# Four tiles of the input projection from attention's hosts into two mixed seven-product pairs

## The chip, the core and the metric

The kernel runs on one core of one Trainium2 chip, as one launch. The metric is the device time of the launch in microseconds. The core has TensorE (PE, matrix products into PSUM), VectorE (DVE), ScalarE (ACT), GpSimd (POOL), SyncE (SP, which here issues most of the DMAs), and 16 DMA engines that move data between device memory and SBUF.

## The reference, cut to what matters

One step of a streaming encoder layer on 1024 prompt frames and 32 sample frames, model width 1024, in float32:

```python
h = rms_norm(x, g_mix)
z = h @ w_in
q, k, v, ch, cb, cc, ga, gb = jnp.split(z, SPLITS, axis=-1)
a = attn_core(q, k, v) @ w_attn_out           # 16 heads of 64, 4 key heads, window of chunks, sink
u = cc * ch
up = jnp.concatenate([conv_left, u], axis=1)
conv = sum(up[:, j:j + n] * conv_w[j] for j in range(3))
bo = (cb * conv) @ w_conv_out
x = x + (jax.nn.sigmoid(ga) * a + jax.nn.sigmoid(gb) * bo) @ w_mix_out
x = x + memory_attention(rms_norm(x, g_cross))
x = x + jnp.square(jax.nn.relu(rms_norm(x, g_mlp) @ w_up)) @ w_down
```

The layer also returns the new keys and values and the last two rows of `u` (the conv state).

## The kernel before, in words

Activations lie transposed: 128 features in the partitions, frames in the free dimension. The 1056 frames are three chunks of 384, 384 and 288 (`CH`, chunks 0 to 2). The 1024 features are eight blocks of 128. A weight tile holds the 1024 input features of 128 output features, 512 KB.

Each float32 value is used as a high part (cast to fp32r by ACT) and a low part (what is left, by DVE). A block product is three matmuls: high by high, high by low, low by high. So a whole tile on one chunk is 8 x 3 = 24 matmuls (`gemm`, L195), and on the three chunks 72: 48 of 384 columns, 24 of 288. The casts and subtractions of a weight tile are L129 and L130 (`split`); `issue_w` (L164) makes them, with `fetch_w` (L147) loading the tile ahead through SP. For a few weight tiles that are used once per chunk the low part is written to device memory at the first use and read back later (`kept`, L1824; the write is L179, the read L172, and the high part is cast at L173).

The input projection has 50 such tiles: 8 of queries, 2 of keys (values apart), and 8 each of conv H, B and C, gate a and gate b. They are treated in two ways.

*Hosts.* Attention consists of 36 units (4 key heads by 9: eight blocks of 128 prompt queries and one of sample queries; `Unit`, L558). A unit has three steps: `scores` (products, then bias and maximum on DVE, exponentials on ACT, and the multiplication by the reciprocal sum, shared between ACT and DVE), `turn` (transposes on PE at L616, split into high and low), and `values` (products, then a sum). Whole tiles are laid between these steps, so that PE has work while DVE and ACT work on a softmax. These tiles are the hosts: a list of 20 at L765, three slots each (one per chunk). `begin` (L774) gives the slot in which each unit's scores start; its transposes come two slots later, its values three. Conv tiles of blocks 0 to 3, queries of key heads 1 to 3, the second key tile and gate a of block 0 are the hosts.

*Pairs.* The other conv tiles and gates go two output tiles at a time through a scheme with seven half products where eight are usual, on chunks 0 and 1. A product (L903) is 4 blocks x 3 matmuls of 384 columns, so a pair is 84 of these where two whole tiles have 96; chunk 2 is done plainly (`gate_c2`, L933), 24 matmuls of 288 for each tile. The scheme needs combinations of the activations, made beside the output products of attention, and combinations of the two tiles' weights. `CPAIRS` (L727) lists the conv pairs: C, H, B of blocks (4, 5), then of (6, 7). After them come seven pairs of gate a and gate b. In `conv_pair` (L1016) the six results of a pair come in a fixed order: first tile chunk 0, first tile chunk 2, second tile chunk 1, first tile chunk 1, second tile chunk 0, second tile chunk 2. `conv_C`, `conv_H` and `conv_B` take them: C is kept, H is multiplied by it to `u`, and B multiplies the three-tap sum of `u`.

*Weight sums.* POOL makes the weight combinations through `sum_step` (L740): it issues the load of the next half tile, then adds four times (L757) on the one before and issues its store. Two buffers take turns (`sum_tile`, L734): a tile of its own, and the space of `xacc`, in which sums of squares are gathered later. There are 62 pieces: 26 for the pairs, 32 for the down projection, 4 for the up projection. Steps are hung on the hosts (26 of them), on attention's output products, and on the pairs (three each). Their order among themselves is pinned; a timeline model at compile time sets how all other instructions of an engine are ordered between them.

*After the pairs* comes the trunk of chunk 0: eight conv_out tiles (`do_conv_out`, L1192, in which POOL adds the two branches, L1201, except in the last), conv_out tile 0 of chunk 1, and eight mix tiles (`do_mix`, L1207). Then the same for chunk 1 beside the cross attention of chunk 0, and so on.

The lines that the later steps touch: `open_att` (L456, opens attention's buffers), the softmax's multiplications (L606 on ACT, L608 on DVE), the conv state's writes (L681 and L1066), `load_a` (L959, loads attention's output for a gate), `do_attn_out` (L847: where the gate of a block is known, DVE multiplies and the product is stored; else ACT copies and the plain output is stored).

Of the kernel before, what the change touches and what calls it, by code (L numbers as in the profile page):

```python
# [10 lines left out]
F32 = mybir.dt.float32  # L11
# [7 lines left out]
P = 128  # L19
# [21 lines left out]
def hybrid_step(ctx: ExitStack, tc: tile.TileContext, io):  # L41
# [48 lines left out]
    usum_d = dram.tile([2, P, 2, 2, 512], F32, name="usum_d")  # L90
    gsum_d = dram.tile([13, P, 2, 2, 512], F32, name="gsum_d")
    a_d = spill("a_d")
# [362 lines left out]

    def open_att():  # L456
        closed(st_cm)
        A["cm"], A["pool"] = opened("att", bufs=1, reuse_waits="tile", side="right")
        A["cvt"] = A["pool"].tile([P, 4, 4], F32, name="cvt")

# [97 lines left out]
    class Unit:  # L558
# [5 lines left out]
        def scores(self):  # L564
# [39 lines left out]
            for h in range(G):  # L604
                if h < G // 2:
                    act.mul(stl[:, h, :nk], stl[:, h, :nk], rec[:, h : h + 1])  # L606
                else:
                    dve.tensor_scalar_mul(stl[:, h, :nk], stl[:, h, :nk], rec[:, h : h + 1])  # L608
# [31 lines left out]
    def do_conv(which, f, extras=()):  # L640
        def fn(w):
# [35 lines left out]
            if which == "H":  # L677
                pool_e.tensor_copy(A["cvt"][:, f, 0:2], u[:, 1024:1026])
                pool_e.tensor_copy(A["cvt"][:, f, 2:4], u[:, 1058:1060])
                if f == 3:  # L680
                    sp.dma_start(io["o_conv"][:, :4], A["cvt"])  # L681

# [43 lines left out]
    HBC = {"H": 0, "B": 1, "C": 2}  # L726
    CPAIRS = [(which, f) for f in (4, 6) for which in "CHB"]  # L727
    ptiles = [(10 + 8 * HBC[which] + f, 11 + 8 * HBC[which] + f) for which, f in CPAIRS]
    ptiles += [(34 + f, 42 + f) for f in PAIRS]
# [35 lines left out]
    hosts = []  # L765
    conv = [(which, f) for f in range(4) for which in "CHB"]
    take = lambda n: [conv.pop(0) for _ in range(n)]
    hosts += take(3) + [("Q", 1, 0), ("Q", 1, 1)]
    hosts += [("K", 1)] + take(2) + [("Q", 2, 0), ("Q", 2, 1)]
    hosts += take(3) + [("Q", 3, 0), ("Q", 3, 1)]  # L770
    hosts += take(4) + [("G", 0)]
    assert not conv and len(hosts) == 20

    begin = [[1, 2, 3, 5, 6, 8, 10, 11, 13]] + [[0, 1, 3, 5, 6, 8, 10, 11, 13]] * 2 + [[0, 1, 3, 4, 6, 7, 9, 10, 12]]  # L774
    slots = [[[], [], [], []] for _ in range(3 * len(hosts) + 1)]
    for kv in range(KV):
        o = 15 * kv
        slots[max(o - 2, 0)][2].append(lambda kv=kv: do_KS(kv))
        slots[o + 1][0].append(lambda kv=kv: do_KC(kv))
        for p in range(9):  # L780
            u = Unit(kv, p)
            at = o + begin[kv][p]
            slots[at][3].append(u.scores)
            slots[at + 2][1].append(u.turn)
            slots[at + 3][0].append(u.values)
    for i, h in enumerate(hosts):
# [8 lines left out]
        if h[0] == "Q":  # L795
            fn, key = do_Q(h[1], h[2], extras), qt(h[1], h[2])
        elif h[0] == "K":
            fn, key = do_K(h[1], extras), ("w_in", 8 + h[1])
        elif h[0] == "G":
            fn, key = do_gate(lambda c, t: sa.__setitem__((c, 0), t), extras), ("w_in", 34)  # L800
        else:
            fn, key = do_conv(*h, extras), conv_w(h[1], h[0])
# [175 lines left out]
    def conv_H(f, c, x, s):  # L978
        n = CH[c][1]
        t = ct2[f, c]  # L980
        u = cu[f, c] = slot(G["pool"], f"Gb{c}", n, F32)
        if s is None:
            dve.tensor_mul(u, x, t)
        else:
            dve.tensor_sub(u, x, s)
            dve.tensor_mul(u, u, t)
        if c == 2:
            pool_e.tensor_copy(cvt[0][:, f - 4, 0:2], u[:, 254:256])
            pool_e.tensor_copy(cvt[0][:, f - 4, 2:4], u[:, 286:288])

    def conv_B(f, c, x, s):
# [22 lines left out]
        sp.dma_start(bc_d[c][:, f], b)  # L1014

    def conv_pair(i):  # L1016
        which, f = CPAIRS[i]
        t1, t2 = ptiles[i]
        out = {"C": conv_C, "H": conv_H, "B": conv_B}[which]
        op = lambda kind: [gop[kind, k] for k in range(4)]  # L1020
        w1 = take_w(("w_in", t1))
        if i == 0:
# [3 lines left out]
            pump(4)  # L1026
        A1, B, C = (acc_tile([P, 384]) for _ in range(3))
        product(A1, w1, 0, op("b11"), True)
        s1 = Y["top"].tile([P, 384], F32, tag="s1", name=nm("s1"))
# [3 lines left out]
        product(A1, w1, 1, op("b21"), False)  # L1033
        out(f, 0, A1, None)
        pump(0)
        out(f, 2, gate_c2(w1), None)
        issue_w()
# [10 lines left out]
        product(B, w3, 0, op("n3"), False)  # L1048
        out(f + 1, 1, B, v)
        sum_step()  # L1050
        product(C, w4, 1, op("b22"), False)
        out(f, 1, C, u2)
        issue_w()
        fetch_w()
        w2 = take_w(("w_in", t2))
        product(B, w2, 1, op("n4"), False)
        out(f + 1, 0, B, s1)
        sum_step()
        issue_w()
        fetch_w()  # L1060
        out(f + 1, 2, gate_c2(w2), None)
        if i == len(CPAIRS) - 1:
            load_a(1, 0)
            load_a(1, 2)
        if which == "H" and f + 1 == NF - 1:
            sp.dma_start(io["o_conv"][:, 4:], cvt[0])  # L1066
# [756 lines left out]
    for name, n in (("w_conv_out", NF), ("w_mix", NF), ("w_cq", 2), ("w_co", 2)):  # L1823
        kept.update(((name, j), None) for j in range(1, n, 2) if (name, j) not in (("w_conv_out", 3), ("w_conv_out", 5)))  # L1824

# [355 lines left out]
```

## Time and profile before

| what | value |
|---|---|
| device time, median of 3 runs | 1732.54 us (1732.36 to 1736.21) |
| profiled execution | 1732.39 us |
| its span, first to last instruction | 1730.6 us |
| attention with its 20 hosts | 83.5 to 405.3 us |
| gate b of block 0, three short products, then attention's output products | 405.3 to 518.9 us |
| six conv pairs, seven gate pairs | 518.9 to 784.9 us |
| conv_out and mix of chunk 0 | 784.9 to 857.0 us |
| DMA traffic | 365.48 MB, mean 211 GB/s |

The page gives busy times and the costliest groups; the windows view gives busy times by stage, the granted PE clock and the DMA share; the timeline gives single instructions with the idle time before them and what ended it (`[1.83 <-DMA ...]`). Matmuls are pipelined: a matmul of 384 columns is drawn with 0.34 us, but the next one starts about 0.17 us after it, so costs are read from start to start.

### The profile page before, as it was taken

The numbers are of one execution on the slowest core, as the hardware profiler recorded it, in microseconds if no ns is written. First come the engines' busy times: TensorE is split into PE (matmuls) and PEld (weight loads), VectorE is DVE, ScalarE is ACT, GpSimd is POOL, SyncE is SP. The second block draws the span as 40 slices with busy tenths as digits, with TensorE's granted clock in tenths as the row PEclk, the third lists the DMA queues.
The fourth block names the chain that finished last, engine by engine and source line by source line (L and its number), as shares of the span: only waits on it lengthen the run. The fifth ranks groups of instructions, "written<-read, shape, count | busy, mean of one in ns | idle before, by whom it ended". The sixth has DMA issues, their size and how long they took to land.

```text
span 1730.6 us, 32544 instructions
## 1 busy us (share of the span) xinstructions
PE 1711.4 (99%) x12166; PEld 1694.8 (98%) x12166; DVE 1221.3 (71%) x2282; ACT 892.8 (52%) x1748; POOL 643.9 (37%) x731
## 2 busy tenths in 40 slices
PE   9999999999999999999999999999999999999998
PEld 8999999999999999999999999999999999999998
DVE  7788797986647776546777889787666686555675
ACT  8676666665223223434556676765444463433444
POOL 0024667675445554462225142106565410000122
PEclk9999999999999999999999999999999999999999
DMA  5334444547886768877766667776666695555554
GB/s 187 99 110 153 128 153 158 173 147 245 277 308 228 255 228 284 283 251 242 260 210 202 223 229 257 239 247 212 223 219 220 212 324 184 192 185 174 191 172 162
DMA packets 185566, 365.48 MB, mean 211 GB/s; under 512 B 19760, under 2 KB 102352, under 8 KB 185280
## 3 DMA queue, kind: packets, MB, share of 16 engines
q1 hardware_dynamic: 165376, 296.37, 51.8%
q0 software_dynamic: 19408, 66.27, 11.1%
q8 instruction: 95, 1.56, 0.4%
q10 hardware_dynamic: 624, 0.77, 0.1%
q14 instruction: 63, 0.52, 0.1%
HBM read 263.31 MB, written 99.43 MB: 210 GB/s over the span
## 4 chain that ended last, share of the span: by engine, by line
PE 42%; DMA 5%; DVE 3%; ACT 1%; issue 1%; POOL 0%; DVEq 0%; ACTq 0%; SPq 0%; POOLq 0%
PE acc L1954 5%; PE acc L1952 5%; PE acc L1953 5%; PE acc L908 4%; PE acc L909 4%; PE acc L910 4%; PE acc L202 2%; PE acc L200 2%; PE acc L201 2%; PE pc L908 2%; PE pc L910 2%; PE pc L909 2%; DMA wr<-wsum_d 1%; DVE wl L130 1%; DMA ct<-m_d 1%
## 5 line engine op out<-in xcount | busy, mean ns | idle before, releaser
L129 ACT CAST wh<-wr 128x1024 fp32r<-128x1024 f32 (+1 forms) x226 | 236.4, 1046 | 397.6 <-PE acc L1953 119.8
L130 DVE TENSOR_TENSOR wl<-wr,wh 128x1024 fp32r<-128x1024 f32 (+1 forms) x226 | 290.8, 1287 | 109.6 <-ACT wh L129 108.2
L287 POOL TENSOR_TENSOR xacc<-xacc,ct 128x384 f32<-128x384 f32 (+1 forms) x55 | 75.1, 1370 | 361.7 <-ACT ct L285 359.9
L200 PE MATMUL acc<-X,wh 128*128 128x384 f32 (+1 forms) x576 | 188.3, 327 | 0.0
L201 PE MATMUL acc<-X,wh 128*128 128x384 f32 (+1 forms) x576 | 187.2, 325 | 0.5 <-DVE X L291 0.5
L202 PE MATMUL acc<-X,wl 128*128 128x384 f32 (+1 forms) x576 | 186.0, 323 | 0.0
L200 PE MATMUL acc<-Y,wh 128*128 128x384 f32 (+1 forms) x432 | 140.6, 325 | 1.9 <-DVE ct L1200 1.9
L202 PE MATMUL acc<-Y,wl 128*128 128x384 f32 (+1 forms) x432 | 140.1, 325 | 1.8 <-DMA wl<-wl_d 1.8
L201 PE MATMUL acc<-Y,wh 128*128 128x384 f32 (+1 forms) x432 | 140.0, 324 | 0.0
L757 POOL TENSOR_TENSOR xacc<-xacc 128x256 f32<-128x256 f32 x124 | 110.2, 889 | 7.1
L201 PEld LDWEIGHTS acc<-X,wh 128*128 128x128 f32 x576 | 108.5, 188 | 2.1 <-DVE X L291 0.8
L200 PEld LDWEIGHTS acc<-X,wh 128*128 128x128 f32 x576 | 108.4, 188 | 0.8
L202 PEld LDWEIGHTS acc<-X,wl 128*128 128x128 f32 x576 | 108.4, 188 | 0.7
L757 POOL TENSOR_TENSOR ws<-ws 128x256 f32<-128x256 f32 x124 | 103.0, 831 | 7.4
L1954 PE MATMUL acc<-n,wl 128*128 128x264 f32 x352 | 100.1, 285 | 0.2 <-DVE wl L130 0.2
L1952 PE MATMUL acc<-n,wh 128*128 128x264 f32 x352 | 100.3, 285 | 0.0
L1953 PE MATMUL acc<-n,wh 128*128 128x264 f32 x352 | 100.2, 285 | 0.0
L200 PEld LDWEIGHTS acc<-Y,wh 128*128 128x128 f32 x432 | 81.7, 189 | 2.8 <-DVE ct L1200 2.8
L202 PEld LDWEIGHTS acc<-Y,wl 128*128 128x128 f32 x432 | 81.7, 189 | 2.1 <-DMA wl<-wl_d 2.1
L201 PEld LDWEIGHTS acc<-Y,wh 128*128 128x128 f32 x432 | 81.6, 189 | 0.0
L599 ACT ACTIVATE S<-S,nmx 128x257 f32<-128x257 f32 (+1 forms) x132 | 64.4, 490 | 25.8 <-DVE nmx L594 24.8
L908 PE MATMUL acc<-n,wh 128*128 128x264 f32 x256 | 72.9, 285 | 0.0
(474 smaller groups left out, 5999.1 us busy)
## 6 DMA issues: line engine op xcount, KB each, us to landing
wr<-in_w_up SPq DMA_DIRECT2D x53, 512.0 KB, 4.3
wr<-in_w_in SPq DMA_DIRECT2D x52, 512.0 KB, 4.0
wr<-wsum_d SPq DMA_DIRECT2D x40, 512.0 KB, 3.5
wr<-gsum_d SPq DMA_DIRECT2D x26, 512.0 KB, 4.5
wr<-in_w_conv_out SPq DMA_DIRECT2D x24, 512.0 KB, 4.1
wr<-in_w_mix SPq DMA_DIRECT2D x24, 512.0 KB, 4.9
wr<-in_w_down SPq DMA_DIRECT2D x24, 512.0 KB, 3.6
n_d<-Z SPq DMA_DIRECT2D x32, 264.0 KB, 4.3
```

Of the source, the lines that this page charges most:

```text
L129: act.copy(hi, src)
L130: dve.tensor_sub(lo, src, hi.bitcast(F32))
L200: pe.matmul(out, wh[:, a], hi, start=(k == 0), stop=False)
L201: pe.matmul(out, wh[:, a], lo, start=False, stop=False)
L202: pe.matmul(out, wl[:, a], hi, start=False, stop=(k == len(acts) - 1))
L757: pin(pool_e.tensor_tensor(t[:, to], t[:, x], t[:, y], op=ALU.add))
L908: pe.matmul(acc, wh[:, a], hi, start=(start and k == 0), stop=False, skip_group_check=True)
L909: pe.matmul(acc, wh[:, a], lo, start=False, stop=False, skip_group_check=True)
L910: pe.matmul(acc, wl[:, a], hi, start=False, stop=(k == 3), skip_group_check=True)
L1952: pe.matmul(a, wh[:, s], hi, start=(t == 0 and k == 0), stop=False, skip_group_check=True)
L1953: pe.matmul(a, wh[:, s], lo, start=False, stop=False, skip_group_check=True)
L1954: pe.matmul(a, wl[:, s], hi, start=False, stop=(t == 1 and k == 7), skip_group_check=True)
```

## The change

- The hosts are 16 instead of 20: C, H and B of block 3 and gate a of block 0 leave the list. `begin` packs a key head's nine units into 12 slots instead of 15. The very first unit has three slots before its transposes instead of two.
- Two pairs stand ahead of the six: (C of block 3, H of block 3), and (B of block 3, gate a of block 0). They bring four more pieces for POOL. `conv_pair` takes a kind for each of its two tiles. In the first new pair, H on chunk 1 comes before C on chunk 1, so its multiplication is put off until C is there (`late`). Gate a is multiplied by attention's output, loaded at the start of its pair (`gate_a`).
- The conv state of block 3 is stored by SP from `u` itself, instead of through POOL's copies.
- In a unit of four heads ACT does three of the four multiplications by the reciprocal sum, instead of two.
- `open_att` starts with an exponential of one column, scaled by zero.
- conv_out tile 1 leaves `kept`: its low part is subtracted anew for each chunk.

```diff
-    gsum_d = dram.tile([13, P, 2, 2, 512], F32, name="gsum_d")
+    gsum_d = dram.tile([15, P, 2, 2, 512], F32, name="gsum_d")
...
     def open_att():
+        act.activation(warm[0], mrc[:, :1], AF.Exp, scale=0.0)
         closed(st_cm)
...
-                if h < G // 2:
+                if h < G - 1:
                     act.mul(stl[:, h, :nk], stl[:, h, :nk], rec[:, h : h + 1])
...
-    CPAIRS = [(which, f) for f in (4, 6) for which in "CHB"]
-    ptiles = [(10 + 8 * HBC[which] + f, 11 + 8 * HBC[which] + f) for which, f in CPAIRS]
+    CPAIRS = [("C", 3, "H", 3), ("B", 3, "a", 0)] + [(which, f, which, f + 1) for f in (4, 6) for which in "CHB"]
+    w_col = lambda which, f: 34 if which == "a" else 10 + 8 * HBC[which] + f
+    ptiles = [(w_col(*at[:2]), w_col(*at[2:])) for at in CPAIRS]
...
-    conv = [(which, f) for f in range(4) for which in "CHB"]
+    conv = [(which, f) for f in range(3) for which in "CHB"]
     take = lambda n: [conv.pop(0) for _ in range(n)]
-    hosts += take(3) + [("Q", 1, 0), ("Q", 1, 1)]
-    hosts += [("K", 1)] + take(2) + [("Q", 2, 0), ("Q", 2, 1)]
-    hosts += take(3) + [("Q", 3, 0), ("Q", 3, 1)]
-    hosts += take(4) + [("G", 0)]
-    assert not conv and len(hosts) == 20
-
-    begin = [[1, 2, 3, 5, 6, 8, 10, 11, 13]] + [[0, 1, 3, 5, 6, 8, 10, 11, 13]] * 2 + [[0, 1, 3, 4, 6, 7, 9, 10, 12]]
+    hosts += take(2) + [("Q", 1, 0), ("Q", 1, 1)]
+    hosts += [("K", 1)] + take(1) + [("Q", 2, 0), ("Q", 2, 1)]
+    hosts += take(2) + [("Q", 3, 0), ("Q", 3, 1)]
+    hosts += take(4)
+    assert not conv and len(hosts) == 16
+
+    begin = [[1, 3, 4, 5, 6, 7, 8, 9, 10]] + [[0, 1, 2, 4, 5, 6, 8, 9, 10]] * 2 + [[0, 1, 2, 3, 4, 6, 7, 8, 9]]
...
-        o = 15 * kv
+        o = 12 * kv
...
-            slots[at + 2][1].append(u.turn)
-            slots[at + 3][0].append(u.values)
+            lag = 3 if kv == p == 0 else 2
+            slots[at + lag][1].append(u.turn)
+            slots[at + lag + 1][0].append(u.values)
...
+            if t is None:
+                return lambda: dve.tensor_mul(u, u, ct2[f, c])
             dve.tensor_mul(u, u, t)
-        if c == 2:
+        if c == 2 and f == 3:
+            sp.dma_start(io["o_conv"][:, 3, 0:2], u[:, 254:256])
+            sp.dma_start(io["o_conv"][:, 3, 2:4], u[:, 286:288])
+        elif c == 2:
...
+    def gate_a(f, c, x, s):
+        t = tmp(CH[c][1])
+        if c == 2:
+            dve.tensor_mul(t, x, R[2])
+        else:
+            dve.tensor_sub(t, x, s)
+        act.activation(t, t, AF.Sigmoid)
+        dve.tensor_mul(t, t, la[f, c])
+        sp.dma_start(m1_d[c][:, f], t)
...
+        if CPAIRS[i][2] == "a":
+            load_a(0, 1)
+            load_a(0, 0)
+            load_a(0, 2)
         product(A1, w1, 0, op("b11"), True)
...
         product(C, w4, 1, op("b22"), False)
-        out(f, 1, C, u2)
+        out(0, 1, C, u2)
+        for fn in late:
+            if fn:
+                fn()
...
-        kept.update(((name, j), None) for j in range(1, n, 2) if (name, j) not in (("w_conv_out", 3), ("w_conv_out", 5)))
+        kept.update(((name, j), None) for j in range(1, n, 2) if (name, j) not in (("w_conv_out", 1), ("w_conv_out", 3), ("w_conv_out", 5)))
```

More of the change, by code (lines that the diff above doesn't have):

```diff
@@ L456, in open_att @@
     def open_att():
+        act.activation(warm[0], mrc[:, :1], AF.Exp, scale=0.0)
         closed(st_cm)
         A["cm"], A["pool"] = opened("att", bufs=1, reuse_waits="tile", side="right")
-        A["cvt"] = A["pool"].tile([P, 4, 4], F32, name="cvt")
+        A["cvt"] = A["pool"].tile([P, 3, 4], F32, name="cvt")
     def at_tile(shape, dt, tag, bufs=1):
@@ L679, in fn @@
                 pool_e.tensor_copy(A["cvt"][:, f, 2:4], u[:, 1058:1060])
-                if f == 3:
-                    sp.dma_start(io["o_conv"][:, :4], A["cvt"])
+                if f == 2:
+                    sp.dma_start(io["o_conv"][:, :3], A["cvt"])
         return fn
@@ L798, in hybrid_step @@
             fn, key = do_K(h[1], extras), ("w_in", 8 + h[1])
-        elif h[0] == "G":
-            fn, key = do_gate(lambda c, t: sa.__setitem__((c, 0), t), extras), ("w_in", 34)
         else:
@@ L979, in conv_H @@
         n = CH[c][1]
-        t = ct2[f, c]
+        t = ct2.get((f, c))
         u = cu[f, c] = slot(G["pool"], f"Gb{c}", n, F32)
@@ L1014, in conv_B, with out @@
         sp.dma_start(bc_d[c][:, f], b)
+    def gate_a(f, c, x, s):
[7 more added lines that the diff above has]
+        sp.dma_start(m1_d[c][:, f], t)
     def conv_pair(i):
-        which, f = CPAIRS[i]
         t1, t2 = ptiles[i]
-        out = {"C": conv_C, "H": conv_H, "B": conv_B}[which]
+        outs = {"C": conv_C, "H": conv_H, "B": conv_B, "a": gate_a}
+        late = []
+        def out(e, c, x, s):
+            kind, f = CPAIRS[i][2 * e : 2 * e + 2]
+            late.append(outs[kind](f, c, x, s))
         op = lambda kind: [gop[kind, k] for k in range(4)]
@@ L1033, in conv_pair @@
         product(A1, w1, 1, op("b21"), False)
-        out(f, 0, A1, None)
+        out(0, 0, A1, None)
         pump(0)
-        out(f, 2, gate_c2(w1), None)
+        out(0, 2, gate_c2(w1), None)
         issue_w()
@@ L1048, in conv_pair @@
         product(B, w3, 0, op("n3"), False)
-        out(f + 1, 1, B, v)
+        out(1, 1, B, v)
         sum_step()
         product(C, w4, 1, op("b22"), False)
-        out(f, 1, C, u2)
+        out(0, 1, C, u2)
+        for fn in late:
+            if fn:
+                fn()
         issue_w()
@@ L1056, in conv_pair @@
         product(B, w2, 1, op("n4"), False)
-        out(f + 1, 0, B, s1)
+        out(1, 0, B, s1)
         sum_step()
@@ L1060, in conv_pair @@
         fetch_w()
-        out(f + 1, 2, gate_c2(w2), None)
+        out(1, 2, gate_c2(w2), None)
         if i == len(CPAIRS) - 1:
@@ L1064, in conv_pair @@
             load_a(1, 2)
-        if which == "H" and f + 1 == NF - 1:
+        if CPAIRS[i][2:] == ("H", NF - 1):
             sp.dma_start(io["o_conv"][:, 4:], cvt[0])
```

## The prediction

> **What bounds the kernel now.** I read the engine shares of the page first, then the windows by stage, then the timelines round the few places where TensorE (PE) pauses.
>
> ```profile
> span 1730.6 us, 32544 instructions
> PE 1711.4 (99%) x12166; PEld 1694.8 (98%) x12166; DVE 1221.3 (71%) x2282; ACT 892.8 (52%) x1748; POOL 643.9 (37%) x731
> ```
>
> PE is busy for 99% of the span, so a matmul that is not issued shortens the kernel, and other work matters only where it makes PE wait. The stages that the change touches are attention with its hosts, the output products of attention, the conv pairs, and the first chunk of conv_out and mix (columns: us, busy time of PE, weight loads, DVE, ACT, POOL, granted clock, DMA share, GB/s):
>
> ```profile
> 83.50:405.30 321.80, 320.67 (x2099) 312.79 (x2097) 264.92 (x677) 209.08 (x531) 185.47 (x268) 1.00 0.46 149
> 423.20:518.90 95.70, 95.70 (x603) 95.70 (x602) 54.99 (x81) 29.92 (x58) 43.94 (x58) 1.00 0.86 297
> 518.90:668.40 149.50, 147.82 (x927) 147.59 (x925) 108.43 (x171) 46.87 (x67) 77.17 (x110) 1.00 0.71 244
> 784.90:857.00 72.10, 71.49 (x410) 70.96 (x409) 47.00 (x70) 35.88 (x61) 18.96 (x13) 1.00 0.80 268
> ```
>
> PE is idle for 1.1 us in attention, never beside the output products, 1.7 us in the pairs and 0.6 us in the first trunk stage. DVE is 82% busy in attention (264.92 of 321.80), ACT 65%. So the change can win its matmuls and a few pauses, and can lose wherever a helper falls behind.
>
> **Part 1: seven products for eight.** Four tiles (C, H and B of feature block 3, gate a of block 0) leave the hosts and become two pairs. Two whole tiles and one pair are to be priced:
>
> ```profile
> 405.26 0.39 PE L200 MATMUL acc<-X,wh 128*128 128x384 f32 x1
> 416.86 0.30 PE L200 MATMUL pa<-X,wh 128*128 128x288 f32 x1
> 610.47 0.34 PE L908 MATMUL acc<-X,wh 128*128 128x384 f32 x1
> 631.52 0.34 PE L908 MATMUL acc<-X,wh 128*128 128x384 f32 x1
> ```
>
> The first two rows are the first matmul of a whole tile (48 matmuls of 384 columns, 24 of 288) and the first one after it: 11.60 us. The other two stand one pair apart (84 of 384, 48 of 288): 21.05 us. Four tiles cost 46.4 us and go; two pairs cost 42.1 us and come. **Term: -4.3 us.** Nothing hides it, since PE is the bound on both sides.
>
> What comes with the two pairs: eight weight tiles to cast and subtract instead of four, the three loads of attention's output for gate a, two small writes of the conv state, and the elementwise work of the four tiles; attention's first output tile is copied out by ACT where DVE multiplied it by the gate. The pairs' stage has room: DVE 108.43 of 149.50 us, DMA share 0.71, while the output products show no PE idle at a DMA share of 0.86. I take 0; without that cover it is the one pause that the stage has now:
>
> ```profile
> 532.57 0.40 PE L202 MATMUL pa<-X,wl 128*128 128x288 f32 x1 [1.68 <-DVE wl L130]
> 520.00:560.00 40.00, 38.32 (x241) 38.09 (x240) 28.31 (x42) 14.47 (x24) 20.80 (x31) 1.00 0.68 234
> ```
>
> It falls in the first pair, where DVE also splits the stored operands. The new first pair has the same splits in the same place, so I keep the 1.7 us; it could go or double (-1.7 to +1.7).
>
> **Part 2: attention in 16 hosts.** The 36 units lose 46.4 us of the 321.8 us that they lay beside; 275.4 us remain. The helpers (groups between 76 and 425 us, then two hosts by windows):
>
> ```profile
> L130 DVE TENSOR_TENSOR wl<-wr,wh 128x1024 fp32r<-128x1024 f32 x26 | 35.1, 1351 | 9.0 <-ACT wh L129 8.8
> L608 DVE TENSOR_SCALAR S<-S,rec 128x256 f32<-128x256 f32 x60 | 28.5, 513 | 0.8
> L669 DVE SCALAR_TENSOR_TENSOR ct<-u,prm,ct 128x384 f32<-128x384 f32 x16 | 10.4, 649 | 0.8 <-ACT ct L667 0.7
> L669 DVE SCALAR_TENSOR_TENSOR ct<-u,prm,ct 128x290 f32<-128x290 f32 x8 | 5.0, 623 | 0.0
> L606 ACT ACTIVATE S<-S,rec 128x256 f32<-128x256 f32 x56 | 25.5, 504 | 8.6 <-DVE rec L603 8.5
> L129 ACT CAST wh<-wr 128x1024 fp32r<-128x1024 f32 x25 | 26.2, 1047 | 15.5 <-PE acc L201 10.9 <-DMA wr<-in_w_in 3.0 <-PE mv L211 1.6
> 244.70:260.70 16.00, 15.65 (x103) 15.00 (x102) 15.34 (x42) 11.47 (x34) 10.65 (x14) 1.00 0.42 133
> 358.50:375.60 17.10, 17.10 (x115) 16.64 (x114) 15.83 (x41) 12.59 (x32) 14.04 (x20) 1.00 0.44 138
> ```
>
> DVE loses four weight subtractions (5.4 us), the taps of one of the four B tiles (15.4 / 4 = 3.9 us), and one normalising multiply in each of the 28 four-head units of 256 keys, at 28.5 / 60 = 0.475 us (13.3 us), which goes to ACT at 25.5 / 56 = 0.455 us (12.7 us). I leave out the smaller multiplications, so this is an upper side: DVE 264.9 - 22.6 = 242.3 of 275.4 us, 88%. ACT, with four weight casts of 1.05 us less: 209.1 + 12.7 - 4.2 = 217.6, 79%. The last two rows are the densest hosts of now: at 15.83 of 17.10 (93%) PE does not wait, at 15.34 of 16.00 (96%) it waits 0.35 us. The first key head is the tight one: seven of its full units begin in consecutive slots. I price its four hosts like the 96% one: 4 x 0.35 = **+1.4 us**. Bounds: 0, and all 16 hosts like it, 5.6 us.
>
> The first unit gets its exponential table loaded early, and one slot more before its transposes:
>
> ```profile
> 96.38 1.28 ACT L599 ACT_TABLE_LOAD   x1 [1.35 <-DVE nmx L594]
> 100.08 0.30 PE L616 MATMUL pt<-ident,S 128*128 128x128 f32 x1 [0.79 <-issue]
> ```
>
> The 1.28 us load lies in the first softmax, and PE then pauses 0.79 us before the first transpose. **Term: -0.8 us** (bounds -0.8 and 0); next late there is nothing, as the lag alone gives a whole slot.
>
> **Part 3: the low part of conv_out tile 1 formed afresh.** Now it is written to DRAM at its first use and read back for the other chunks:
>
> ```profile
> 852.54 0.53 SPq L172 DMA_DIRECT2D wl<-wl_d  x1
> 853.07 1.05 ACT L173 CAST wh<-wr 128x1024 fp32r<-128x1024 f32 x1 [2.44 <-PE acc L202]
> 859.41 0.44 PE L202 MATMUL acc<-Y,wl 128*128 128x384 f32 x1 [1.83 <-DMA wl<-wl_d]
> 860.00:861.00 1.00, 1.00 (x8) 1.00 (x7) 1.00 (x2) 0.45 (x1) 0.00 (x0) 0.97 0.09 35
> 861.00:862.00 1.00, 1.00 (x5) 1.00 (x4) 1.00 (x2) 1.00 (x4) 0.28 (x1) 0.50 0.03 12
> 864.00:865.00 1.00, 1.00 (x6) 1.00 (x6) 1.00 (x2) 1.00 (x3) 0.00 (x0) 0.83 0.49 170
> ```
>
> The read is issued at 852.54, and PE waits 1.83 us for it. The high part is cast by 854.1; a subtraction of 1.35 us behind it ends near 855.5, two us before PE asks (859.41 - 1.83 = 857.58). The wait goes: **-1.8 us** (bounds -1.8 and 0). Right after the pause the granted clock is 0.97, then 0.50 for three us, then 0.83: 0.03 + 1.5 + 0.17 = 1.7 us of PE time. I take this half clock as the pause's consequence, **-1.7 us** (bounds -1.7 and 0); against it, the 1.68 us pause of the first pair left the clock at 1.00. By the Trainium skill ("TensorE: Matmul & The Clock Gate", Part 1) the clock halves only after an idle window of about 3.4 us; a 1.83 us pause would then not be the cause, and the sum would keep the 1.7 us. That is one of the rivals.
>
> The two added subtractions lie beside conv_out of chunks 1 and 2; DVE is busy 47.00 of 72.10 us in the stage ahead of it, so they cost nothing.
>
> **Part 4: POOL's weight sums.** Each pair adds two sum steps (loads, four adds, stores): 66 for 62. Six fewer are hung on attention's hosts (20 for 26).
>
> ```profile
> L757 POOL TENSOR_TENSOR xacc<-xacc 128x256 f32<-128x256 f32 x48 | 41.3, 860 | 2.4
> L757 POOL TENSOR_TENSOR ws<-ws 128x256 f32<-128x256 f32 x44 | 35.2, 801 | 2.3
> L757 POOL TENSOR_TENSOR xacc<-xacc 128x256 f32<-128x256 f32 x76 | 69.0, 908 | 4.7
> L757 POOL TENSOR_TENSOR ws<-ws 128x256 f32<-128x256 f32 x80 | 67.8, 848 | 5.1
> L752 POOL DMA_DIRECT2D xacc<-in_w_down x16 | 8.6, 538 | 68.4 <-DMA wsum_d<-xacc 63.1 <-DMA gsum_d<-xacc 5.3
> 773.44 1.46 POOL L761 DMA_DIRECT2D usum_d<-ws  x2 [0.41 <-POOL ws L757]
> 790.02 1.00 POOL L1201 TENSOR_TENSOR ct<-ct,ct 128x384 f32<-128x384 f32 x1 [15.13 <-DMA wr<-in_w_conv_out]
> ```
>
> The first two rows end at 405.3: 92 adds, 23 steps done, three behind the 26 given out in program order. The next two are the other 39, until 774.9: (774.9 - 405.3) / 39 = 9.5 us each, of which 68.4 / 16 = 4.3 us is POOL waiting for the store of the step before. So POOL goes at its own pace, and now ends 15 us ahead of its first conv_out add. With the change 17 steps are done at 358.9; 49 x 9.5 = 465 us more end at about 824, while the products end at about 781. Some four steps come to lie beside conv_out of chunk 0. PE idles 0.61 us in that stage now; I take twice that, **+1.2 us**, with bounds 0 and the price below.
>
> **Sum.** -4.3 - 1.8 - 1.7 - 0.8 + 1.4 + 1.2 = -6.0 us. The profiled execution took 1732.39 us with a span of 1730.6 and 1.8 us around it; that gives 1726.4, and the median of the runs shown is 0.15 us higher: 1726.5 us, 0.35% less. About 0.3% (5.2 us) is what a measurement of this kernel can tell from no change.
>
> **Rivals.** First, POOL's tail blocks the trunk: **slower**. POOL runs in order; an add of conv_out behind a sum step waits for that step's store and adds, up to 4.3 + 3.5 = 7.8 us. The slot that it frees is what SP's next load waits for, and the weights queue behind that load:
>
> ```profile
> SPq L1196 <- POOL ct L1201: 10.0, 6, 2.1
> 812.89 0.38 SPq L159 DMA_DIRECT2D wr<-in_w_mix  x1
> 822.65 0.34 PE L200 MATMUL acc<-M,wh 128*128 128x384 f32 x1
> wr<-in_w_mix SPq DMA_DIRECT2D x24, 512.0 KB, 4.9
> ```
>
> SP already waits six times for these adds, 2.1 us at most. A weight tile is asked for 9.8 us ahead of its first matmul, of which 4.9 + 1.05 + 1.35 = 7.3 go on landing, cast and subtraction: 2.5 us to spare. So each of four steps can cost 5.3 us, 21 us in all: -8.6 + 1.4 + 21 = +14, 1746 us. It decides from 3.1 us a step (+12.4, where the sum reaches +5.2). For it: the tail must go somewhere. Against it: POOL's other instructions are placed between the steps now, so an add need not stand behind a whole one. 20%: 13 slower, 7 within 0.3%.
>
> Second, attention becomes bound by DVE and ACT: 5.6 us for 1.4, net -1.8, 1730.7 us. For it: ACT rises from 65% to 79% while DVE stays above 82%. Against it: the hosts at 93 and 96%. 15%: 12 within 0.3%, 3 slower (where the waits pile up).
>
> Third, the half clock comes whatever the pause: -4.3, 1728.2 us, within 0.3%. 8%; the pause and the dip stand side by side once.
>
> Fourth, the change does not do what it says at conv_out tile 1, since DVE comes as late as the read did: both terms stay, -2.5, 1730.0 us. 5%, within 0.3%; DVE has 2 us to spare there.
>
> **The numbers.** The forecast keeps 52%, faster. Within 0.3%: 7 + 12 + 8 + 5 = 32%. Slower: 16%. The range begins at 1722.0 (all gains, the first pair's pause gone as well: -8.6 - 1.7 = -10.3) and ends at 1738.0, which takes in rivals two to four and the lower half of the first.
>
> **What would show it.** Right: attention's stage, first host to last, near 277 us with PE idle under 3 us; two pairs of about 21 us; no wait for a stored low part at the first conv_out tile 1 of chunk 1, and clock 1.00 there; the last sum store 35 to 50 us later against the products' end than now. Wrong: PE pauses between the first conv_out and the last mix of chunk 0, with SP waiting for POOL's adds longer than 2.5 us; pauses before transposes in the first key head; a half clock at another place.

## The result, and the profile after

| | before | after |
|---|---|---|
| median, both measured together | 1733.08 us (6 runs) | 1778.81 us (6 runs, 1762.39 to 1782.77) |
| ratio after / before | | 1.0231, 95% interval 1.0201 to 1.0261 |
| profiled execution | 1732.39 us | 1782.77 us |
| its span | 1730.6 us | 1781.0 us |

The change makes the kernel 2.3% slower. The forecast was 1726.5 us in a range of 1722 to 1738. The first rival's mechanism came true at a higher price: it had put the wait at 21 us, conv_out alone lost 34.5, and the pairs, which the rival did not name, lost some 15 more. The profiled execution is the longest of the six, so the numbers below, place by place, are an upper side; experiments have profiles of their own, which differ from their medians by up to 6.5 us.

From the page of after: span, PE's share, the granted clock in 40 slices of 44.5 us, and one group of matmuls.

```profile
span 1781.0 us, 32576 instructions
PE 1720.9 (97%) x12142; PEld 1698.7 (95%) x12142; DVE 1227.0 (69%) x2271; ACT 911.0 (51%) x1791; POOL 658.6 (37%) x752
...
PEclk9999999999999989997999999999999999999999
...
L200 PE MATMUL acc<-Y,wh 128*128 128x384 f32 (+1 forms) x432 | 143.3, 332 | 31.1 <-DVE ct L1228 29.4
```

PE falls from 99% to 97%, the clock dips in two places (slices 15 and 19), and a single group, the high-by-high matmuls of conv_out, has waited 29.4 us for DVE. Next the windows of after by stage, with the columns of the prediction: attention's hosts, output products, pairs, conv_out, mix.

```profile
83.80:358.70 274.90, 274.69 (x1806) 266.20 (x1805) 231.01 (x620) 210.84 (x551) 134.65 (x207) 1.00 0.43 136
377.00:472.70 95.70, 95.70 (x602) 95.70 (x602) 57.29 (x77) 29.52 (x58) 53.05 (x67) 1.00 0.85 284
472.70:793.80 321.10, 309.50 (x1911) 308.32 (x1910) 201.92 (x302) 104.72 (x155) 165.95 (x211) 0.98 0.73 243
793.80:866.10 72.30, 43.39 (x217) 41.70 (x215) 29.19 (x36) 18.30 (x29) 41.55 (x52) 0.81 0.67 231
866.10:900.10 34.00, 33.76 (x192) 33.20 (x193) 24.14 (x36) 17.47 (x33) 8.59 (x7) 1.00 0.70 243
```

Put against before by the first matmul of each stage, and at the end by the last one: until the pairs 46.2 us are won (518.9 against 472.7); the pairs take 55.1 us more (321.1 against 266.0), where two pairs of 21.05 us were bought with it; conv_out of chunk 0 takes 34.5 more (72.3 against 37.8); mix 0.2 less; everything behind 7.2 more (875.0 against 867.8). The sum is 50.4 us, which is the difference of the spans.

So there are two holes. The timeline of after, rows of PE that ended a pause (in the text such a pause is read from the start of the last matmul before it to the start of the next, 0.3 us more than the idle time in the row):

```profile
653.31 0.69 PE L909 MATMUL acc<-X,wh 128*128 128x384 f32 x1 [10.87 <-ACT wh L129]
...
832.04 0.66 PE L200 MATMUL acc<-Y,wh 128*128 128x384 f32 x1 [21.33 <-DVE ct L1228]
```

Neither ACT nor DVE is the cause; both stood in a queue behind it. What SP's queue waited for, first between 620 and 660 us, then between 780 and 850, and under it the same for before between 618 and 680:

```profile
SPq L1094 <- POOL cvt L995: 25.8, 1, 25.8
```

```profile
SPq L1224 <- POOL ct L1229: 31.4, 3, 29.3
```

```profile
SPq L1066 <- POOL cvt L989: 11.4, 1, 11.4
```

The first is the store of the conv state (`out_o_conv`, L1094; L1066 in before): SP issues it, and it waits for small copies that POOL makes. The second is the load of `m1` for a conv_out tile; it needs a slot that POOL's addition (L1229) frees. Behind each stand the weight loads, because SP issues in order. POOL's and SP's timelines of after round the second hole show both queues:

```profile
813.59 0.57 POOL L765 DMA_DIRECT2D wsum_d<-ws  x1 [0.41 <-POOL ws L759]
816.97 1.43 POOL L752 DMA_DIRECT2D ws<-in_w_up  x2 [2.80 <-DMA wsum_d<-ws]
818.42 3.14 POOL L759 TENSOR_TENSOR xacc<-xacc 128x256 f32<-128x256 f32 x4
821.97 1.46 POOL L763 DMA_DIRECT2D usum_d<-xacc  x2 [0.41 <-POOL xacc L759]
826.13 1.46 POOL L752 DMA_DIRECT2D xacc<-in_w_up  x2 [2.70 <-DMA usum_d<-xacc]
827.60 0.73 POOL L759 TENSOR_TENSOR ws<-ws 128x256 f32<-128x256 f32 x1
828.28 1.00 POOL L1229 TENSOR_TENSOR ct<-ct,ct 128x384 f32<-128x384 f32 x1
```

```profile
798.48 0.34 SPq L159 DMA_DIRECT2D wr<-in_w_conv_out  x1
798.87 1.11 SPq L844 DMA_DIRECT2D ct<-bc_d  x2
829.31 0.32 SPq L1224 DMA_DIRECT2D ct<-m_d  x1
829.73 0.38 SPq L159 DMA_DIRECT2D wr<-in_w_conv_out  x1
```

The first conv_out addition runs at 828.28, in the middle of a sum step and behind several whole ones. SP issues nothing from 799.98 to 829.31, and the next weight tile only then. The order of POOL's instructions was fixed at compile time, with the addition at a place in the chain that the chip reached some 29 us after SP needed it; that the compile-time model had the chain further ahead is inferred, not shown. The last store of the chain is issued at 774.2 us in before and at 853.7 in after, 60 us behind the last product.

### The profile page after: what moved, and what is told of

Its sections match the earlier page's. It is cut to its first block, busy times and chain, and to the rows that moved or that the text cites. A ratio compares the mean times of both kernels' runs of the same rounds, so it can differ in the third digit from the quotient of the medians.

```text
span 1781.0 us, 32576 instructions
## 1 busy us (share of the span) xinstructions
PE 1720.9 (97%) x12142; PEld 1698.7 (95%) x12142; DVE 1227.0 (69%) x2271; ACT 911.0 (51%) x1791; POOL 658.6 (37%) x752
## 5 line engine op out<-in xcount | busy, mean ns | idle before, releaser
L129 ACT CAST wh<-wr 128x1024 fp32r<-128x1024 f32 (+1 forms) x232 | 242.3, 1045 | 434.7 <-PE acc L1981 130.2
L130 DVE TENSOR_TENSOR wl<-wr,wh 128x1024 fp32r<-128x1024 f32 (+1 forms) x232 | 297.5, 1283 | 126.2 <-ACT wh L129 124.6
L200 PE MATMUL acc<-Y,wh 128*128 128x384 f32 (+1 forms) x432 | 143.3, 332 | 31.1 <-DVE ct L1228 29.4
L200 PE MATMUL acc<-X,wh 128*128 128x384 f32 (+1 forms) x480 | 157.5, 328 | 0.0
L201 PE MATMUL acc<-X,wh 128*128 128x384 f32 (+1 forms) x480 | 156.4, 326 | 0.0
L202 PE MATMUL acc<-X,wl 128*128 128x384 f32 (+1 forms) x480 | 156.2, 326 | 0.0
L759 POOL TENSOR_TENSOR xacc<-xacc 128x256 f32<-128x256 f32 x132 | 117.5, 890 | 7.5
L759 POOL TENSOR_TENSOR ws<-ws 128x256 f32<-128x256 f32 x132 | 115.7, 876 | 7.6
L1980 PE MATMUL acc<-n,wh 128*128 128x264 f32 x352 | 100.3, 285 | 0.4 <-ACT wh L129 0.4
L1981 PE MATMUL acc<-n,wh 128*128 128x264 f32 x352 | 100.1, 284 | 0.0
L909 PE MATMUL acc<-X,wh 128*128 128x384 f32 x240 | 81.2, 339 | 10.9 <-ACT wh L129 10.9
L201 PEld LDWEIGHTS acc<-X,wh 128*128 128x128 f32 x480 | 90.4, 188 | 0.9
L200 PEld LDWEIGHTS acc<-X,wh 128*128 128x128 f32 x480 | 90.3, 188 | 0.7
L202 PEld LDWEIGHTS acc<-X,wl 128*128 128x128 f32 x480 | 90.3, 188 | 0.6
L910 PE MATMUL acc<-X,wh 128*128 128x384 f32 x240 | 81.2, 338 | 0.0
```

The costliest lines, as they stand in the source:

```text
L129: act.copy(hi, src)
L130: dve.tensor_sub(lo, src, hi.bitcast(F32))
L200: pe.matmul(out, wh[:, a], hi, start=(k == 0), stop=False)
L201: pe.matmul(out, wh[:, a], lo, start=False, stop=False)
L202: pe.matmul(out, wl[:, a], hi, start=False, stop=(k == len(acts) - 1))
L759: pin(pool_e.tensor_tensor(t[:, to], t[:, x], t[:, y], op=ALU.add))
```

## The experiments

Each was run with the kernel before on the same chip. All ratios are against before, with their 95% interval.

**One cause at a time (a_store, a_dve, a_both).** The first takes the conv state's store off SP's queue, the second takes chunk 0's additions off POOL, the third does both.

```diff
-            sp.dma_start(io["o_conv"][:, 4:], cvt[0])
+            pool_e.dma_start(io["o_conv"][:, 4:], cvt[0])     # a_store, a_both
...
-            (dve if f == NF - 1 else pool_e).tensor_tensor(t, t, t1, op=ALU.add)
+            (dve if c == 0 or f == NF - 1 else pool_e).tensor_tensor(t, t, t1, op=ALU.add)     # a_dve, a_both
```

> The changed kernel, but the store of the conv state that SP held back until POOL's copies were done is issued by POOL itself. Theory (POOL's sum chain runs later than the order laid out at compile time, and whoever stands behind a POOL instruction waits for whole sum steps): SP no longer stops at this store, so the 11.0 us pause of PE in the last B pair and the half clock behind it go; but POOL's chain ends no earlier (about 850 us), so the first add of conv_out comes as late as now and PE's 21.5 us pause there grows by about what was won: time within 6 us of the changed kernel's. Rival (the weights come late because the DMA engines are full): the pause in the last B pair stays near 11 us, time the same to 2 us.

> The changed kernel, with chunk 0's conv_out additions on DVE instead of POOL. Theory: nothing of conv_out stands behind POOL's sum steps, so the pauses of 21.5 and 5.5 us there go (34.6 us over that stage). What is late next is the space of the square sums, which POOL's chain holds until about 850 us: the first squares of mix would come at about 837 us and stop ACT for some 15 us. Net about 20 to 30 us faster than the changed kernel, 1750 to 1760 us. Rival (the conv_out stage pauses because its weights or the attention branch's loads are late): the stage stays 72 us long and the time at 1779 us.

> The changed kernel with both edits: store of the conv state from POOL, chunk 0's additions on DVE. Theory: the pause in the last B pair and those in conv_out go, and the end of POOL's chain sets how long mix waits for the space of the square sums: about the time of the additions on DVE alone, 1745 to 1757 us, with the pause now at the first mix tiles. Rival (two independent causes that add): 12.7 + 34.6 us less than the changed kernel, 1731 us.

Measured: a_store 1776.11 us, 1.0262 (1.0223 to 1.0301); a_dve 1754.07 us, 1.0119 (1.0088 to 1.0151); a_both 1763.2 us, 1.0175 (1.0143 to 1.0208), above what was expected of it. The pairs of a_store, then SP's waits in its conv_out:

```profile
472.70:779.00 306.30, 306.30 (x1911) 306.30 (x1910) 195.20 (x302) 104.51 (x155) 161.23 (x206) 1.00 0.74 251
```

```profile
SPq L1224 <- POOL ct L1229: 39.5, 3, 37.5
```

Without SP's store the pairs have no PE idle at all and cost 306.3 us, 40.3 more than in before, for 42.1 bought. Part of what a_store wins in the pairs is lost again at once: PE comes to conv_out 14.6 us earlier, but POOL's chain ends only 5.7 us earlier (848.7 against 854.4), SP waits 37.5 us instead of 29.3, and conv_out takes 78.9 us instead of 72.3. a_dve keeps the first pause (8.0 us at 642.3) and shortens conv_out to 42.6 us, but mix then takes 43.2. a_both shows the same once more: it mends both places and is slower than a_dve. With no addition of chunk 0 left on POOL, conv_out takes 40.7 us, and then a single one of chunk 1 (conv_out tile 0) is enough; mix takes 58 us. The space of the square sums, which had been expected to hold mix up, is not what is waited for. The waits of a_both between 830 and 860 us:

```profile
DVE M L130 <- ACT M L129: 24.1, 2, 23.5
ACT M L129 <- POOL ct L1229: 23.6, 1, 23.6
...
PE acc L200 <- DVE Ga L1243: 19.9, 1, 19.9
```

ACT and DVE, in order as well, stand behind that one addition for 23.5 us, and PE for 19.9. The chain ends at 853.0 in it. The two holes are one debt: mending a place moves the wait to the next one that needs POOL.

**The tail alone, in the kernel before (b_tail).** Six idle sum steps are put into before's list, and nothing else.

```diff
+    pieces[26:26] = [("x", 0, q) for q in range(6)]
```

> The kernel before, with six idle sum steps more on POOL, which load a down-projection piece again and store it to a place that nothing reads. Hosts, pairs and matmuls stay those of before. Theory: POOL's chain ends 57 us later, about 832 us, 47 us into the trunk, and its conv_out additions come behind it: pauses in conv_out of 10 to 40 us, 1743 to 1773 us. Rival (the new pairs or the denser hosts are the cause, not the length of POOL's chain): the time of before, 1733 us, to 3 us.

Measured: 1762.64 us, 1.0177 (1.0131 to 1.0223); the chain ends at 832.7, PE pauses 15.1 us at 802.8. SP's waits in b_tail between 780 and 840 us (its lines lie two further down than before's):

```profile
SPq L1198 <- POOL ct L1203: 24.6, 3, 20.5
```

A later chain without any other part of the change gives the same hole. That settles the cause of the larger one. The size follows too. Where POOL makes the additions, conv_out takes 37.7 us as long as the chain ends no later than 2.6 us behind its start (nine kernels); with the chain 34 us behind that start it loses 20.7 us (a_more, below), with 46 us 23.5 (b_tail), with 61 us 34.6 (after), with 70 us 41.2 (a_store).

**The change with a shorter chain (a_short), and with steps shared out otherwise (a_more).** a_short copies the last ten of the down projection's pieces as they are, without sums. a_more hangs 25 steps on the 16 hosts.

```diff
+    W["plain"] = pieces[-14:-4]     # a_short: before the four of the up projection
...
-        if i > 4 and i % 2:
+        if i > 4:                   # a_more
             extras.append((2, sum_step))
```

> The changed kernel with the last ten of the 32 pieces of the down projection's weights copied by DMA as they are instead of being added up (their sums are left out, so the second half's products are not those of the reference). This takes ten steps out of POOL's chain and changes nothing else. Theory: the chain ends near 757 us, ahead of conv_out; all pauses at the last B pair, in conv_out and at the first mix go, and what is left is the change without POOL's tail: between 1725 us (4.3 + 0.8 + 3.5 us less than before) and 1732 us (if the rest of the kernel keeps the 3 to 7 us that it is longer by). Rival (the pairs' stage or the trunk pauses for another cause as well): over 1740 us.

> The changed kernel with 25 sum steps hung on the 16 hosts instead of 20, at the same places of the program otherwise. Theory: if POOL can keep that pace beside the units, the chain ends some 50 us earlier, about 805 us, still 10 to 25 us into conv_out: 20 to 40 us faster than the changed kernel, 1740 to 1760 us. Rival (in attention each step waits for its stores and for the units' own POOL work, so POOL cannot go faster there): the chain ends at 840 us or later, and the time stays above 1765 us.

Measured: a_short 1742.5 us, 1.0051 (1.0034 to 1.0068), over the 1725 to 1732 us expected: the chain ends at 778.0 (757 was expected), conv_out takes 37.7 us and mix 33.1, with no pause over 1 us in either. What is left is the pause at the conv state's store (10.7 us at 642.3, half clock until 657.0) and 3 us behind the trunk. a_more 1764.71 us, 1.0196 (1.0166 to 1.0227), between its theory and its rival: the chain ends at 823.6, conv_out takes 58.5 us, PE still pauses 17.5 us at 806.3, and the stretch from attention to the pairs takes 4 us more. Hanging more steps on the hosts is no way out.

**The low part alone (b_kept), and the store alone (b_store), in the kernel before.**

```diff
-(("w_conv_out", 3), ("w_conv_out", 5))
+(("w_conv_out", 1), ("w_conv_out", 3), ("w_conv_out", 5))     # b_kept
...
-            sp.dma_start(io["o_conv"][:, 4:], cvt[0])
+            pool_e.dma_start(io["o_conv"][:, 4:], cvt[0])     # b_store
```

> The kernel before with one edit of the change alone: the low part of conv_out tile 1 is subtracted anew for each chunk instead of stored and read back. As forecast: the 1.83 us pause at 857 us goes, and with it the half clock of 1.7 us: 3.5 us less, 1730 us. Rival (the half clock comes at some place anyway): 1.8 us less. Rival (DVE cannot take the two added subtractions where they fall): no gain, or a loss of some us in the second and third chunk.

> The kernel before with the conv state's last store issued by POOL instead of SP. In the profiled execution of before SP waits 11.4 us at this store without a pause of PE, and in the kernel with the one low part formed afresh, whose POOL order is the same up to there, it waits 24.6 us with a pause of 7.9 us. Theory: before stands just short of that pause in most executions and falls into it in some: the median stays within 3 us, and the spread over the executions (1730 to 1740 us) becomes narrower. Rival (the store has no part in it): nothing changes.

Measured: b_kept 1737.95 us, 1.0027 (1.0015 to 1.0038). The pause behind mix and its half clock are gone (no PE idle and a clock of 1.00 in the 10 us from 865.7 us on, where conv_out of chunk 1 goes on), yet the kernel is slower, for two reasons. The stretch behind mix is not shorter for it (868.0 us in the profile, 867.8 in before's with 3.5 us of pause and half clock in it): what goes at its start is lost further on. And the pairs' stage is 8.7 us longer in the profile. SP's waits of b_kept between 618 and 660 us:

```profile
SPq L1066 <- POOL cvt L989: 24.6, 1, 24.6
```

In before SP stood 11.4 us at this store and PE did not notice; here POOL's chain ran 10 us later, SP stood 24.6 us, and PE paused 7.9 us at 646.2. The chain fell behind step by step between about 480 and 600 us; why is open. b_store took 1730.66 us, 0.9982 (0.9970 to 0.9995). Off SP's queue, the store no longer holds up any weight load: SP's wait for POOL's copies is gone from its profile.

**Moving ten of the sums out of the chain (a_late, a_end, a_end_kept).** All three issue the conv state's store on POOL. Ten pieces of the down projection are summed in the up projection's pairs (a_late) or in the first three stages of the down projection (a_end); a_end_kept is a_end with the low part of conv_out tile 1 stored and read back as before.

```diff
+    late_pieces = pieces[-10:]
+    del pieces[-10:]
...
+        if i:                                   # a_late, in up_pair; late_sum follows in it
+            late_load()
...
+                if kind in KINDS[:3]:           # a_end, a_end_kept, in the down projection's products
+                    (late_sum if n % 2 else late_load)()
```

> The changed kernel with those ten pieces moved: POOL loads, adds and stores them one by one in the up projection's second half, through a single buffer, well ahead of their use; the conv state's last store is issued by POOL. Theory: POOL's chain ends ahead of conv_out, and the moved steps lie where POOL is idle for half the time or more: the time of the kernel with the ten sums left out, to 3 us. Rival (POOL's own sums of the up projection come late behind the moved steps): pauses in the up projection, over 1740 us.

> The changed kernel; the last ten down-projection pieces are summed by POOL during the first three stages of the down projection, where POOL is nearly idle, through a single buffer; the conv state's last store is issued by POOL. Theory: with POOL's chain ended ahead of conv_out and no queue behind the conv state's copies, the change is left with its own terms: 1724 to 1731 us, 0.2 to 0.5% faster than before. Rival (moved sums disturb the place they are moved to): pauses in the down projection, 1735 us or more.

> The same kernel with the low part of conv_out tile 1 stored and read back again, as before. If forming it afresh is worth the pause of 1.83 us and the half clock of 1.7 us: 3.5 us slower than its neighbour. If it only moves the pause to the second and third chunk, where the kernel before with this edit alone had about 4 us more idle time between 960 and 1000 us: the same to 1 us, or faster.

Measured: a_late 1745.95 us, 1.0078 (1.0059 to 1.0096); a_end 1747.75 us, 1.0085 (1.0068 to 1.0102); a_end_kept 1743.44 us, 1.0055 (1.0038 to 1.0073). All three missed what was expected of a move that works. In all three the trunk is whole (conv_out 37.7 us, mix 33.1), but behind it 12 to 17.5 us are lost: 885.3, 885.1 and 880.0 us against 867.8. a_end was to have no sums in the up projection. POOL's timeline of a_end shows that it had:

```profile
1127.96 0.53 POOL L742 DMA_DIRECT2D ws<-in_w_down  x1 [6.59 <-DMA wsum_d<-ws]
1132.97 3.77 POOL L749 TENSOR_TENSOR ws<-ws 128x256 f32<-128x256 f32 x4 [4.48 <-DMA ws<-in_w_down]
...
1140.50 0.53 POOL L742 DMA_DIRECT2D ws<-in_w_down  x1 [2.77 <-DMA wsum_d<-ws]
1146.75 5.07 POOL L749 TENSOR_TENSOR ws<-ws 128x256 f32<-128x256 f32 x4 [5.72 <-DMA ws<-in_w_down]
```

All ten ran between 1109 and 1282 us. They depended on nothing later, so the compile-time order could put them into the up projection, and did; POOL stood in front of that stage's work for loads and stores. The move had failed, not the idea.

**The move done by data (a_down, a_down_afresh).** Eight pieces are moved, and the first late load overwrites a tile that has taken one column from an operand of the down projection's second stage. So it cannot run earlier. a_down keeps the low part stored as in before; a_down_afresh forms it anew as the change does.

```diff
+    late_pieces = pieces[-8:]
+    del pieces[-8:]
...
+            if len(late_pieces) == 7:
+                pool_e.tensor_copy(t[:, 0, 0:1], dn["b21", 0][1][:, 0:1].bitcast(F32))
+            pool_e.dma_start(t, io["w_down"][at])
...
-            sp.dma_start(io["o_conv"][:, 4:], cvt[0])
+            pool_e.dma_start(io["o_conv"][:, 4:], cvt[0])
...
+                if kind in KINDS[1:3] or kind == KINDS[0] and n > 1:
+                    (late_sum if n % 2 else late_load)()
```

> The changed kernel with the conv-state store issued by GpSimd, the low part of conv_out's tile 1 stored and read back as before, and the last eight down-projection sums moved behind the up projection: their first load waits for data that only the down projection brings in, so they cannot drift forward as those of the version with late sums did (they ran from 1109 us there). Theory (the added products are worth their 4 us, and all the loss is lateness of GpSimd's chain): the chain ends near 775 us, no pause over 2 us at 642 or between 780 and 850, the stretch behind the trunk is back to 868 to 870 us, span 1724 to 1728, 1726 to 1730 us against 1733 of before, ratio 0.996 to 0.999. Rival (the late sums were not what cost the 12 to 17 us behind the trunk in the version with late sums; something in the change loads that stretch): it stays over 876 us and the time at 1738 or more. Rival two (the weight sums now come late to the down projection): pauses between 1440 and 1560 us.

> As the run beside it, but with the low part of conv_out's tile 1 formed afresh, as the change has it. If forming it afresh costs behind the trunk (the low part's subtractions lie on VectorE where chunk 2 needs it, 960 to 1000 us) more than the pause at 857 us that it removes: 1 to 4 us slower than the run beside it, with more lost between 955 and 1000 us. If the loss there in earlier runs came from the late sums or the late store: 1 to 3 us faster, since the pause behind mix's first tile is gone.

Measured: a_down 1726.3 us, 0.9962 (0.9945 to 0.9980), faster than both kernels; a_down_afresh 1731.52 us, 0.9989 (0.9973 to 1.0006). The windows of a_down by stage (hosts, pairs, conv_out and mix, the rest):

```profile
83.80:359.80 276.00, 275.61 (x1810) 266.80 (x1809) 231.29 (x621) 211.30 (x552) 135.36 (x207) 1.00 0.42 135
...
473.50:781.70 308.20, 306.57 (x1911) 306.32 (x1910) 200.98 (x302) 104.78 (x155) 160.46 (x209) 1.00 0.73 248
781.70:852.50 70.80, 70.80 (x408) 70.80 (x407) 44.72 (x69) 34.44 (x59) 19.32 (x12) 1.00 0.79 266
852.50:1719.00 866.50, 858.69 (x6730) 853.69 (x6729) 613.04 (x1046) 454.92 (x800) 280.05 (x236) 1.00 0.66 224
```

The chain ends at 772.3 us, the trunk has no PE idle, and what lies behind it is back at 866.5 us. The sums of the late pieces are ready in time (last store at 1518.71, and no PE pause over 0.2 us from 1300 us to the last weight product). This is the change's gain without Part 3, with its debt paid in a place where POOL has time. Of the 5.9 us that a_down wins on before, the store off SP's queue brought 2.1 by itself in before (b_store).

Between a_down and its neighbour the stretch behind mix differs by 2.0 us in the profiles (866.5 against 868.5), and the medians by 5.2. PE's waits between 955 and 1000 us, of a_down and then of a_down_afresh:

```profile
PE acc L200 <- DVE ct L1246: 1.5, 2, 0.8
```

```profile
PE acc L200 <- DVE ct L1246: 3.5, 3, 1.5
PE acc L200 <- DVE ct L1310: 1.5, 1, 1.5
PE o L1377 <- ACT PTh L129: 0.7, 1, 0.7
PE o L1377 <- DVE PTl L130: 0.7, 1, 0.7
```

There conv_out of chunk 1, its helpers and chunk 0's cross attention share DVE, and DVE's order comes out otherwise when the low part is formed afresh. That it loses there is shown, and by more than this pair: in the 50 us that begin 100 us behind mix, PE idles 4.7 to 6.6 us in each of the ten profiled kernels that form the low part afresh, and 1.7 to 2.9 us in each of the five that store it. Which of the displaced instructions does it is not settled.

## Why the prediction was wrong, point by point

**The step that failed is Part 4's term, +1.2 us** for POOL's longer chain of weight sums. In its place came 34.5 us in conv_out, and some 15 in the pairs, which the prediction had at 0. Three statements failed in it.

First, the length of the tail. All 49 steps left after the hosts were priced at 9.5 us, the mean of a stretch in which 32 of 39 were steps of the down projection. POOL's groups of after, from 358.7 to 509.6 us (steps of the pairs) and from 509.6 to 814.3 us (steps of the down projection):

```profile
L763 POOL DMA_DIRECT2D gsum_d<-ws x14 | 10.3, 735 | 3.1 <-POOL ws L759 2.9 <-issue 0.3
L763 POOL DMA_DIRECT2D gsum_d<-xacc x12 | 8.8, 734 | 2.5 <-POOL xacc L759 2.4
L752 POOL DMA_DIRECT2D ws<-in_w_in x12 | 8.8, 731 | 29.8 <-DMA gsum_d<-ws 29.8
L752 POOL DMA_DIRECT2D xacc<-in_w_in x12 | 8.8, 731 | 21.6 <-DMA gsum_d<-xacc 21.6
```

```profile
L765 POOL DMA_DIRECT2D wsum_d<-xacc x16 | 9.2, 576 | 6.4 <-POOL xacc L759 6.4
...
L754 POOL DMA_DIRECT2D ws<-in_w_down x16 | 8.6, 539 | 62.7 <-DMA wsum_d<-ws 60.0 <-DMA gsum_d<-ws 2.7
```

A step of the pairs issues two loads and two stores, 1.46 + 1.47 us of POOL's time, where one of the down projection issues one of each, 0.54 + 0.58. The 13 steps took 150.9 / 13 = 11.6 us each, the 32 others 304.7 / 32 = 9.5. The chain ended at 854 us instead of 824; 27 of the 30 us are these 13 steps. The diff's new pieces were all of the dear kind.

Second, "POOL's other instructions are placed between the steps now, so an add need not stand behind a whole one". They are placed between the steps, but at places chosen before the run, for a chain that, it seems, was expected to be done sooner. An in-order engine that is late carries its short instructions with it. The addition was not behind one step but behind as many as the chain was late by: 29.3 us. This would have failed at the forecast length too: a_more's chain ended at 823.6 us, where the prediction had 824, and its conv_out lost 20.7 us, the rival's 21, where the sum had 1.2. At the length that came, the rival's price was too small as well; 34.5 us went in conv_out. What the prediction held against this rival was the wrong sentence.

Third, the first conv_out addition was taken as the first place where POOL's lateness counts. It was the second. SP's store of the conv state needs POOL's copies, and before's own trace has the row, 11.4 us of waiting at L1066; the prediction read SP's waits in the trunk alone. "I take 0" for what comes with the two pairs failed there: the stage took 55.1 us more where 42.1 were bought, by a pause of 11.2 us and the half clock behind it.

The prediction's own sign for the tail did not fit its figures either: 824 against 781, and 774.9 against 784.9 before, put the last sum store 53 us later against the products' end, not 35 to 50. It came 71 us later.

**Part 3, -3.5 us, failed by its place.** Its mechanism was right: in b_kept and a_down_afresh the pause behind mix and the half clock are gone. But the two subtractions were costed at nothing by DVE's load in the stage ahead, not by the stage in which they lie. Against a_down, a_down_afresh loses 2 us in the profiles and 5 in the medians; after idles 6.6 us from 1000 to 1050 us, where before, as far behind its mix, idles 2.3, and its clock is halved for 6.8 us there, which costs 3.4 more. Nor does every kernel that stores the low part have the pause: the profiles of b_store and b_tail show none (0.3 us at most).

**Part 1, -4.3 us, was right.** Whole, undisturbed pairs cost 306.3 us (a_store), 40.3 more than in before, for 46.2 won ahead of them: a net of -5.9. The terms of Parts 1 and 2 gave -3.7 (-4.3 - 0.8 + 1.4); most of the rest is the pause in the first pair, 1.7 us, which the prediction kept and which went.

**Part 2, +1.4 us, was too careful.** Attention's hosts took 274.9 us with 0.2 us of PE idle (275.4 were forecast without a stall), although DVE was 84% and ACT 77% busy. The pause of the first unit is gone, as forecast (-0.8). The second rival did not happen.

The third and the fourth rival did not happen either: with the pause at conv_out tile 1 gone, the half clock is gone, and DVE came in time. So that pause was the half clock's cause, although it was shorter than 3.4 us.

**What the runs leave of the change:** with the chain's tail moved by data, the store off SP's queue and the low part stored, 1726.3 us. That this is the forecast's figure is chance: the kernel takes in two cures and not the change's Part 3.

## What to carry to other kernels

When a background chain on an in-order engine is made longer, look for every short instruction of that engine that others wait for, on all queues, and price each by how late the chain will be there, not by one step of it. Price a chain's steps by kind, counting each DMA that a step issues. Work that is moved to a quieter stage has to be tied there by data; otherwise the compile-time order may bring it forward into a stage that has no room.

## What the runs showed of the hardware

Half clock comes in steps of one length. Windows of after, cut at the three places where its clock is halved in and behind the holes:

```profile
644.90:658.60 13.70, 5.04 (x15) 4.54 (x16) 5.31 (x10) 4.59 (x7) 5.31 (x10) 0.50 0.83 301
815.60:839.50 23.90, 6.87 (x20) 6.39 (x21) 7.45 (x10) 5.18 (x9) 14.59 (x19) 0.50 0.54 183
849.70:853.10 3.40, 3.09 (x10) 3.12 (x11) 1.96 (x4) 0.93 (x2) 2.69 (x3) 0.51 0.78 227
```

The lengths are 1, 4 and 7 times 3.41 us, and the starts lie 170.7 and 34.1 us apart, 50 and 10 times that. The clock falls while PE still pauses (at 644.9; the last matmul before the pause starts at 642.1) and stays down for 5.3 us after work has resumed at 653.3, for 7.5 after 832.0. The Trainium skill ("TensorE: Matmul & The Clock Gate", Part 1) tells of a free-running activity window of 3413 ns, and this trace agrees. By the same Part 1 of the Trainium skill the clock halves after an idle window of about 3.4 us. The long holes agree; pauses shorter than a window went both ways here, and the measurement decides. Two kernels have 2.0 us of PE idle at the same place, where conv_out of chunk 1 follows mix. The windows at its end, of a_end_kept and then of a_down:

```profile
854.00:857.00 3.00, 3.00 (x12) 3.00 (x13) 2.50 (x4) 1.90 (x4) 0.73 (x1) 0.66 0.45 158
```

```profile
855.00:858.00 3.00, 2.79 (x16) 2.79 (x17) 2.27 (x4) 1.67 (x4) 0.50 (x1) 1.00 0.49 168
```

The first ran at 0.66, the second at 1.00. A pause shorter than a window can cost half a window (1.7 us) or nothing, so the 1.7 us that the prediction charged to the 1.83 us pause are not a fixed price. The clock's own changes give the grid of windows in each profile, and with it the two cases part. In a_end_kept the pause (851.94 to 853.95) lies whole in the window from 851.56 to 854.97, 59% of it. In a_down it (853.19 to 855.21) lies across a border at 854.00 and takes 24% of one window and 35% of the next. Before's pause of 1.83 us lies whole in one window (857.52 to 860.93), 54% of it; its pause of 1.68 us in the first pair takes 49% of one. Laid over all fifteen profiles, from 20 us to the last matmul, the grid gives the same: each of the 21 windows at full clock in which PE idles 58% or more is followed by half clock, none in which it idles 31% or less is, and of the 47 between them 8 are. So how much of one window is idle goes far to decide it. What else decides between 31% and 58% is open.
